# Opening of a two-layer decoder kernel: first weight tile in two loads, other order of its cast and products

## The chip, the cores and the metric

The kernel runs on one core of a Trainium2 chip. The metric is the device time of one execution in microseconds (us), lower is better. A core has five engines that run their own instruction streams and wait for each other by semaphores: TensorE (PE; its weight loads stand apart as PEld), VectorE (DVE), ScalarE (ACT), GpSimd (POOL) and SyncE (SP). Sixteen DMA engines, shared by all queues, move data between the chip's main memory and the core's on-chip memory.

## The reference

The input x is 256 x 1024 in float32. Two residual layers follow; each is an RMSNorm, one wide input projection, two groups of attention heads with gates, and an output projection that is added to x:

```
h    = rmsnorm(x, norm_gain[layer])
proj = h @ w_in_ab            # layer 0: 1024 x 4104; layer 1 uses w_in_cd
qa, ka, va, ga, qb, kb, vb, gb, fb = split_cols(proj, AB_SIZES)
...                           # two attentions; y gets their gated outputs
x    = x + y @ w_out_ab
```

What concerns us is the very beginning: the norm of x and the first 1024 columns of `h @ w_in_ab` (qa and ka, 512 columns each).

## The kernel before, in words

**Precision.** Every product is made in three: a float32 matrix is split into a high part (a cast to the engine's fast float32 form, made by ACT) and a low part (raw minus high, made by DVE), and `mm3` (lines 257 to 260) adds high x high, low x high and high x low. So a weight tile takes an ACT cast (line 120) and a DVE subtraction (line 121) before TensorE can use it. Both are in `wload`, which can do a tile in pieces.

**Loads.** All weight tiles are loaded by `wraws` (line 108) on SP's DMA queue, 512 KB each. The norm's scale is not applied to h before the projection, but to its result, so the projection can begin on the transposed x. `h_block(l, t, k, ps)` (lines 218 to 224) takes one transposed 128 x 128 block of x out of PSUM, row half t, column block k, times the norm's gain: ACT writes its high part `hth`, and DVE its low part `htl`.

**The opening** (from line 857 on) is written in program order for all engines. SP loads row half 0 of x (`xload(0)`), weight tile 0 (the rows of block k = 0, 1024 columns), row half 1 of x, tiles 1 to 3, and then tiles 4 to 7 into the rotating buffer `raw`; tiles 0 and 1 stand in the buffer `yth` and tiles 2 and 3 in `ytl`, so the profile calls their loads by these names. Here they are called w0, w1, w2, w3. POOL issues the loads of small parameters and, at line 908, of `wf`: 8 columns of the 1024 rows of w_in_ab, 32 bytes from each row, called the list load here.

`warm(n)` (lines 852 to 855) issues n matmuls of zeros with 512 columns, which nobody reads; `WARM = (5, 3)` says how many come ahead of the transposed gain column (line 875) and behind the four transposes of the first block group (`x_transp(0, 0)`, line 877).

Then come, by program order: `h_block` of blocks 0 and 1 of row half 0; the split of w0 in two pieces of 512 columns; the three products of w0's first piece with row half 0 (`mm_first(0, 0, 0)`); four transposes of row half 1 (line 883); `h_block` of blocks 0 and 1 of row half 1; the products of the second piece with row half 0; the split of w1; the six products of w0 with row half 1; and then w1's blocks, eight transposes, and w2 and w3 in the same way (lines 890 to 904). From line 905 on, a planner (`tick`) issues the work in units, with SP's loads waiting for free buffers.

Of the kernel before, what the change touches and what calls it, by code (L numbers as in the profile page):

```python
# [22 lines left out]
WF = 1040  # L23
NW = 5
AHEAD = 3
WARM = (5, 3)


@with_exitstack
def trunk_kernel(  # L30
# [6 lines left out]
    nc = tc.nc  # L37
    x, out = x[0], out[0]
    w_ab, wo_ab, w_cd, wo_cd = w_in_ab[0], w_out_ab[0], w_in_cd[0], w_out_cd[0]
# [20 lines left out]
    def xload(t):  # L60
        nc.sync.dma_start(xs[:, t, :], x[t * 128:(t + 1) * 128, :])
# [10 lines left out]
    def params(eng, rows):  # L72
        for i in rows:
            g = gains[i]
            eng.dma_start(
                prow[i:i + 1, :].rearrange("o (r d) -> o r d", r=2),
                bass.AP(tensor=g.tensor, offset=g.offset, ap=[[64, 1], [0, 2], [1, 64]]))

    def bcast(eng, name, src, n, t=None):
        t = cst.tile([128, n], F32, name=name) if t is None else t  # L80
        eng.dma_start(t, bass.AP(tensor=src.tensor, offset=src.offset,
                                       ap=[[0, 128], [1, n]]))
        return t
# [14 lines left out]
    def wraws(parts, nk, n, raw=None):  # L98
        if raw is None:
            raw = wraw.tile([128, WF], F32, name="raw")  # L100
        rv = raw[:, 0:nk * n].rearrange("p (k n) -> p k n", k=nk)
        for (c0, src) in parts:
            if isinstance(src, tuple):
                k0, f0 = src
                nc.gpsimd.tensor_copy(rv[:, :, c0:c0 + 4], wf[:, k0:k0 + nk, f0:f0 + 4])
                continue
            m = src.shape[1]
            last["sp"] = nc.sync.dma_start(rv[:, :, c0:c0 + m],
                                           src.rearrange("(k p) n -> p k n", p=128))
        return raw  # L110

    def wload(parts, nk, n, raw=None, pieces=1):
        if raw is None:
            raw = wraws(parts, nk, n)
        hi = wsp.tile([128, WF], F32R, name="whi")
        lo = wsp.tile([128, WF], F32R, name="wlo")
        m = nk * n // pieces
        for i in range(pieces):
            c = slice(i * m, (i + 1) * m)
            last["act"] = nc.scalar.copy(hi[:, c], raw[:, c])  # L120
            last["dve"] = nc.vector.tensor_tensor(out=lo[:, c], in0=raw[:, c], in1=hi[:, c].bitcast(F32),  # L121
                                    op=OP.subtract)
        return (hi[:, 0:nk * n].rearrange("p (k n) -> p k n", k=nk),
                lo[:, 0:nk * n].rearrange("p (k n) -> p k n", k=nk))
# [3 lines left out]
    tiles, wt, units, running = [], [], [], []  # L128
# [3 lines left out]
    def loads(limit):  # L132
        while len(wt) < len(tiles) and len(wt) - at["freed"] < limit:
            wt.append(wload(*tiles[len(wt)]))
# [11 lines left out]
    def tick(n=1):  # L146
        for _ in range(n):
            need, free, fn = units[at["unit"]]
            at["unit"] += 1
            while len(wt) < need:  # L150
                assert len(wt) - at["freed"] < NW
                wt.append(wload(*tiles[len(wt)]))
            fn()
            stages()
            at["freed"] += free
            loads(AHEAD)
# [37 lines left out]
    def x_transp(t, j):  # L194
        ps = pa.tile([128, 4, 128], F32, name="at", tag="ps")
        for i in range(4):
            k = 4 * j + i
            nc.tensor.transpose(ps[:, i, :], xs[:, t, k * 128:(k + 1) * 128], ident)
        return ps
# [18 lines left out]
    def h_block(l, t, k, ps):  # L218
        hth, htl = H["h"]
        c, g = slice(t * 128, (t + 1) * 128), gcol[:, 8 * l + k:8 * l + k + 1]  # L220
        nc.scalar.activation(hth[:, k, c], ps, AF.Copy, scale=g)
        nc.vector.scalar_tensor_tensor(out=htl[:, k, c], in0=ps, scalar=g,
                                       in1=hth[:, k, c].bitcast(F32),
                                       op0=OP.mult, op1=OP.subtract)
# [6 lines left out]
    def norm_r():  # L231
        ss = sml.tile([128, 2], F32, name="n_ss")
        for t in range(2):
            dump = act.tile([128, D], F32, name="yb")
            nc.scalar.activation(dump, xs[:, t, :], AF.Square, accum_out=ss[:, t:t + 1])  # L235
        m = sml.tile([128, 2], F32, name="n_m")
        nc.vector.tensor_scalar(m, ss, 1.0 / D, EPS, op0=OP.mult, op1=OP.add)
        em = sml.tile([128, 2], F32, name="n_em")
        nc.vector.tensor_scalar(em, m, EPS, None, op0=OP.mult)
        H["em"] = em  # L240
        y = rsqrt_tables(m, [128, 2])
        yield
        r = rsqrt_newton(m, y, [128, 2])
        rx = sml.tile([128, 2], F32, name="n_r")
        nc.vector.tensor_copy(rx, r)
        H["rx"] = rx
        yield
        pb = pa.tile([128, 512], F32, name="at", tag="ps")
        for t in range(2):
            nc.tensor.matmul(pb[:, t * 128:(t + 1) * 128], rx[:, t:t + 1].to_broadcast([128, 128]),  # L250
                             ident, start=True, stop=True)
        rb = act.tile([128, 256], F32, name="rb")
        nc.vector.tensor_copy(rb, pb[:, 0:256])
        H["rb"] = rb
# [7 lines left out]
    def bank():  # L262
        pt = pj.tile([128, 512], F32, name="pj", tag="ps")
        return pt
# [385 lines left out]
    def first():  # L650
        return proj2(w_ab, 0, (lambda ps: qk_heads(ps, 8, 0, qk_dst("qa", slice(0, 4))),
                               lambda ps: qk_heads(ps, 8, 4, qk_dst("ka", slice(0, 4)), room=True)))

    mm_first, run_first = first()
# [194 lines left out]

    wz = scr.tile([128, 512], BF16, name="sq", bufs=3)  # L850

    def warm(n):
        pt = bank()
        for _ in range(n):
            nc.tensor.matmul(pt, wz[:, 0:128], wz, start=True, stop=True)

    with tc.manual_schedule():
        nc.vector.memset(wz, 0.0)
        raws = []
        for n in ("yth", "ytl"):  # L860
            r = act.tile([128, 2, 1024], F32, name=n)
            raws += [r[:, 0, :], r[:, 1, :]]
        xload(0)
        wraws(*tiles[0], raws[0])
        xload(1)
        for i in range(1, 4):
            wraws(*tiles[i], raws[i])
        nc.gpsimd.iota(rel, pattern=[[-1, 256]], base=128, channel_multiplier=1,
                       allow_small_or_imprecise_dtypes=True)
        nc.vector.tensor_scalar(ident, rel[:, 0:128], 128.0, None, op0=OP.is_equal)  # L870
        nc.vector.memset(prow, 0.0)
        params(nc.gpsimd, (0, 4, 1, 5))
        warm(WARM[0])
        pgt = pv.tile([128, 512], F32, name="av", tag="ps")
        nc.tensor.transpose(pgt[:, 0:16], grow, ident[0:16, 0:16])
        nc.vector.tensor_copy(gcol, pgt[:, 0:16])
        p0 = x_transp(0, 0)
        warm(WARM[1])
        h_block(0, 0, 0, p0[:, 0, :])
        h_block(0, 0, 1, p0[:, 1, :])  # L880
        wt.append(wload(*tiles[0], raws[0], 2))
        mm_first(0, 0, 0)
        p1 = x_transp(1, 0)
        h_block(0, 1, 0, p1[:, 0, :])
        h_block(0, 1, 1, p1[:, 1, :])
        mm_first(0, 0, 1)
        wt.append(wload(*tiles[1], raws[1], 2))
        for j in range(2):
            mm_first(0, 1, j)
        for k in (2, 3):  # L890
            h_block(0, 0, k, p0[:, k, :])
            h_block(0, 1, k, p1[:, k, :])
        run_first(1)
        p0, p1 = x_transp(0, 1), x_transp(1, 1)
        wt.append(wload(*tiles[2], raws[2], 2))
        for k in (4, 5):
            h_block(0, 0, k, p0[:, k - 4, :])
            h_block(0, 1, k, p1[:, k - 4, :])
        run_first(2)
        wt.append(wload(*tiles[3], raws[3], 2))  # L900
        for k in (6, 7):
            h_block(0, 0, k, p0[:, k - 4, :])
            h_block(0, 1, k, p1[:, k - 4, :])
        run_first(3)
        at["freed"] += 3
        loads(3)
        bfor = bcast(nc.gpsimd, "bfor", b_forget, 8)
        nc.gpsimd.dma_start(wf, w_ab[:, 4096:4104].rearrange("(k p) n -> p k n", p=128))
        g = norm_r()
        next(g)  # L910
        running.append(g)
        at["freed"] += 1
        tick(1)
        biases((0, 1, 2, 3))
        tick(3)
        gain_cols(0)
# [63 lines left out]
```

## Time and profile before

| what | value |
|---|---|
| median of 3 runs | 278.92 us (276.66 to 279.52) |
| the profiled execution | 279.85 us, its span 278.1 us |
| PE busy, share of the span | 267.6 us, 96% |
| DVE busy | 212.2 us, 76% |
| ACT busy | 178.6 us, 64% |
| POOL busy | 7.2 us, 3% |
| chain that ended last | PE 74%, DMA 9%, DVE 8%, ACT 5% |
| granted TensorE clock, mean | 0.992 |

The span goes from the first to the last instruction of the program; the device time has about 1.7 us more around it. A busy PE is not one at its peak: the ends of its records overlap the next product. The chain is the sequence of work that ended last, followed backwards from the end, each step to what released it; work that is not in the chain was waiting for something in it or had time to spare.

### The profile page before, as it was taken

What the parts mean: (1) busy time and instruction counts of PE and PEld (TensorE: products, weight loads), DVE (VectorE), ACT (ScalarE), POOL (GpSimd) and SP (SyncE); (2) the same over time, 40 slices, a digit from 0 to 9 for tenths busy, and PEclk for the clock granted to TensorE, in tenths of its full rate; (3) what the DMA queues carried; (4) which work ended last, traced back from release to release, by engine and by line L of the source; (5) the groups of instructions that cost most, each with busy time, mean ns of one, the idle gap of its engine ahead of it and who ended that gap; (6) DMA issues with size and microseconds to landing.
All of it is one profiled execution on the core that took longest, in us unless ns stands there. A gap on an engine that the chain in (4) does not pass through costs nothing.

```text
span 278.1 us, 4629 instructions
## 1 busy us (share of the span) xinstructions
PE 267.6 (96%) x1665; PEld 225.7 (81%) x1665; DVE 212.2 (76%) x499; ACT 178.6 (64%) x394; POOL 7.2 (3%) x15
## 2 busy tenths in 40 slices
PE   7999999779999999999999999999999999999994
PEld 2876788558998889999788888888987899897784
DVE  2667998287877549999954988776999888698822
ACT  3469572576687557699742845465785798898500
POOL 6000003000000000000000000000000000000000
PEclk9999999979999999999999999999999999999999
DMA  7974864671444472205855367665508125307012
GB/s 238 202 317 128 225 194 150 195 239 24 148 143 116 118 222 78 77 8 165 247 195 165 90 213 242 212 181 182 167 1 272 35 73 175 132 4 222 5 75 76
DMA packets 26297, 41.38 MB, mean 149 GB/s; under 512 B 1665, under 2 KB 13330, under 8 KB 26274
## 3 DMA queue, kind: packets, MB, share of 16 engines
q1 hardware_dynamic: 26050, 41.04, 47.7%
q0 software_dynamic: 192, 0.04, 1.4%
q8 instruction: 13, 0.21, 0.3%
q14 instruction: 10, 0.08, 0.1%
q10 hardware_dynamic: 32, 0.01, 0.0%
HBM read 40.03 MB, written 1.05 MB: 148 GB/s over the span
## 4 chain that ended last, share of the span: by engine, by line
PE 74%; DMA 9%; DVE 8%; ACT 5%; issue 1%; SPq 1%; ACTq 0%
PE pj L258 21%; PE pj L259 20%; PE pj L260 20%; DMA ytl<-in_w_in_ab_dram 5%; DMA raw<-in_w_in_ab_dram 4%; DVE wlo L121 4%; PE at L509 3%; PE av L551 3%; ACT whi L120 2%; PE at L481 2%; PE at L377 2%; PE at L477 1%; DVE qk_m L344 1%; ACT yb L235 1%; DVE klo L395 1%
## 5 line engine op out<-in xcount | busy, mean ns | idle before, releaser
L121 DVE TENSOR_TENSOR wlo<-raw,whi 128x1024 fp32r<-128x1024 f32 (+1 forms) x70 | 85.2, 1223 | 21.8 <-ACT whi L120 18.3
L120 ACT CAST whi<-raw 128x1024 fp32r<-128x1024 f32 (+1 forms) x70 | 72.4, 1048 | 38.0 <-PE pj L259 20.4
L258 PE MATMUL pj<-whi,hth 128*128 128x512 f32 (+2 forms) x192 | 73.7, 384 | 0.6 <-ACT whi L120 0.5
L260 PE MATMUL pj<-wlo,hth 128*128 128x512 f32 (+2 forms) x192 | 71.2, 371 | 0.5 <-DVE wlo L121 0.5
L259 PE MATMUL pj<-whi,htl 128*128 128x512 f32 (+2 forms) x192 | 71.1, 370 | 0.0
L258 PEld LDWEIGHTS pj<-whi,hth 128*128 128x128 f32 x192 | 36.7, 191 | 8.5 <-ACT whi L120 2.0
L260 PEld LDWEIGHTS pj<-wlo,hth 128*128 128x128 f32 x192 | 36.6, 191 | 8.1 <-DVE wlo L121 1.6
L259 PEld LDWEIGHTS pj<-whi,htl 128*128 128x128 f32 x192 | 36.9, 192 | 5.6
L258 PE MATMUL pj<-hth,whi 128*128 128x256 f32 x128 | 37.0, 289 | 0.0
L260 PE MATMUL pj<-htl,whi 128*128 128x256 f32 x128 | 36.0, 281 | 0.0
L259 PE MATMUL pj<-hth,wlo 128*128 128x256 f32 x128 | 35.9, 281 | 0.0
L258 PE MATMUL pj<-whi,yth 128*128 128x512 f32 (+1 forms) x68 | 26.4, 388 | 0.0
L260 PE MATMUL pj<-wlo,yth 128*128 128x512 f32 (+1 forms) x68 | 25.9, 381 | 0.0
L259 PE MATMUL pj<-whi,ytl 128*128 128x512 f32 (+1 forms) x68 | 25.8, 380 | 0.0
L258 PEld LDWEIGHTS pj<-hth,whi 128*128 128x128 f32 x128 | 24.1, 188 | 0.7 <-issue 0.3
L259 PEld LDWEIGHTS pj<-hth,wlo 128*128 128x128 f32 x128 | 24.2, 189 | 0.0
L260 PEld LDWEIGHTS pj<-htl,whi 128*128 128x128 f32 x128 | 24.1, 188 | 0.0
L490 ACT ACTIVATE e<-e,mn 128x128 f32<-128x128 f32 x32 | 12.5, 390 | 8.9 <-DVE mn L486 8.9
L492 ACT ACTIVATE e<-e,mn 128x256 f32<-128x256 f32 x32 | 15.8, 495 | 0.0
L258 PEld LDWEIGHTS pj<-whi,yth 128*128 128x128 f32 x68 | 12.8, 188 | 2.7 <-issue 0.3
L260 PEld LDWEIGHTS pj<-wlo,yth 128*128 128x128 f32 x68 | 12.8, 188 | 2.6
L259 PEld LDWEIGHTS pj<-whi,ytl 128*128 128x128 f32 x68 | 12.8, 188 | 2.5
(167 smaller groups left out, 390.0 us busy)
## 6 DMA issues: line engine op xcount, KB each, us to landing
raw<-in_w_in_ab_dram SPq DMA_DIRECT2D x28, 512.0 KB, 7.9
raw<-in_w_in_cd_dram SPq DMA_DIRECT2D x26, 512.0 KB, 4.5
raw<-in_w_out_ab_dram SPq DMA_DIRECT2D x8, 512.0 KB, 3.7
raw<-in_w_out_cd_dram SPq DMA_DIRECT2D x8, 512.0 KB, 4.6
xs<-in_x_dram SPq DMA_DIRECT2D x2, 512.0 KB, 6.0
yth<-in_w_in_ab_dram SPq DMA_DIRECT2D x2, 512.0 KB, 7.0
ytl<-in_w_in_ab_dram SPq DMA_DIRECT2D x2, 512.0 KB, 12.7
out_dram<-xs SPq DMA_DIRECT2D x3, 256.0 KB, 2.0
```

The costliest lines, as they stand in the source:

```text
L120: last["act"] = nc.scalar.copy(hi[:, c], raw[:, c])
L121: last["dve"] = nc.vector.tensor_tensor(out=lo[:, c], in0=raw[:, c], in1=hi[:, c].bitcast(F32), op=OP.subtract)
L235: nc.scalar.activation(dump, xs[:, t, :], AF.Square, accum_out=ss[:, t:t + 1])
L258: nc.tensor.matmul(ps, ah, bh, start=first, stop=False)
L259: nc.tensor.matmul(ps, al, bh, start=False, stop=False)
L260: nc.tensor.matmul(ps, ah, bl, start=False, stop=last)
L377: nc.tensor.transpose(pt[:, i, :], qns[t][:, i * 128:(i + 1) * 128], ident)
L481: nc.tensor.matmul(scs[b][:, 128:384], q[r[b], i, :], k[r[b], ik, :], start=n == 0, stop=n == 2)
L490: nc.scalar.activation(e[:, 0:128], e[:, 0:128], AF.Exp, bias=mn[:, 0:1], scale=-1.0, accum_out=sm[:, 0:1])
L492: nc.scalar.activation(e[:, 128:384], e[:, 128:384], AF.Exp, bias=mn[:, 1:2], scale=-1.0, accum_out=sm[:, 1:2])
L509: nc.tensor.transpose(pt[:, i * 128:(i + 1) * 128], blocks[j + i], ident)
L551: nc.tensor.matmul(av[64 * b:64 * b + 64, i, t * 128:256], v[:, t, c:c + 64], p, start=t == 0, stop=t == 1)
```

## The change

The first weight tile is loaded by two instructions of 256 KB, one for each 512 columns. The transposes of row half 0 come behind one more zero product of 512 columns, and behind them come two of 512 and three of 128 columns in place of three of 512. `h_block` of block 1 of row half 0 moves from in front of w0's split to between the two blocks of row half 1, and the products of w0's second piece with row half 0 move in front of the transposes of row half 1.

```
-WARM = (5, 3)
+WARM = (5, 2, 3)
...
-    def warm(n):
+    def warm(n, m=0):
         pt = bank()
-        for _ in range(n):
-            nc.tensor.matmul(pt, wz[:, 0:128], wz, start=True, stop=True)
+        for c in (512,) * n + (128,) * m:
+            nc.tensor.matmul(pt[:, 0:c], wz[:, 0:128], wz[:, 0:c], start=True, stop=True)
...
         xload(0)
-        wraws(*tiles[0], raws[0])
+        for j in range(2):
+            nc.sync.dma_start(raws[0][:, j * 512:(j + 1) * 512], w_ab[0:128, j * 512:(j + 1) * 512])
         xload(1)
...
+        warm(1)
         p0 = x_transp(0, 0)
-        warm(WARM[1])
+        warm(*WARM[1:])
         h_block(0, 0, 0, p0[:, 0, :])
-        h_block(0, 0, 1, p0[:, 1, :])
         wt.append(wload(*tiles[0], raws[0], 2))
         mm_first(0, 0, 0)
+        mm_first(0, 0, 1)
         p1 = x_transp(1, 0)
         h_block(0, 1, 0, p1[:, 0, :])
+        h_block(0, 0, 1, p0[:, 1, :])
         h_block(0, 1, 1, p1[:, 1, :])
-        mm_first(0, 0, 1)
         wt.append(wload(*tiles[1], raws[1], 2))
```

## Rows read from the trace of the kernel before

**Rows 1.** Chain of waits, opening: start us, us, what
```profile
2.59 12.75 DMA ytl<-in_w_in_ab_dram
...
15.36 0.63 ACT whi L120
...
18.23 0.52 ACT whi L120
...
42.62 12.01 DMA raw<-in_w_in_ab_dram
```
**Rows 2.** Timeline of PE, 13.8 to 17: start us, us, instruction [idle before <-releaser]
```profile
14.89 1.04 PE L198 MATMUL at<-ident,xs 128*128 128x128 f32 x8
...
16.03 0.50 PE L258 MATMUL pj<-whi,hth 128*128 128x512 f32 x1
```
**Rows 3.** Stretches: us, busy us of each engine, PEclk, DMA share, GB/s
```profile
3.50:5.50 2.00, 1.68 (x8) 1.23 (x8) 0.24 (x2) 0.30 (x1) 2.00 (x4) 1.00 0.98 272
...
9.00:9.50 0.50, 0.50 (x4) 0.50 (x3) 0.00 (x0) 0.02 (x1) 0.00 (x0) 1.00 5.39 279
9.50:11.50 2.00, 2.00 (x7) 1.53 (x7) 1.03 (x3) 1.58 (x4) 0.00 (x0) 1.00 0.71 10
...
58.80:62.10 3.30, 3.30 (x18) 2.59 (x14) 3.18 (x17) 2.10 (x10) 0.00 (x0) 0.50 0.78 245
```
**Rows 4.** DMA queues, 9.0 to 9.8 us: queue, packets, MB, share of 16 engines
```profile
q0 software_dynamic: 16, 0.03, 473.9%
```
**Rows 5.** Timeline of ACT, 4 to 27 us: columns as in rows 2
```profile
5.20 0.37 ACT L221 ACTIVATE hth<-at,gcol 128x128 fp32r<-128x128 f32 x1 [3.18 <-PE at L198]
5.99 0.37 ACT L221 ACTIVATE hth<-at,gcol 128x128 fp32r<-128x128 f32 x1 [0.42 <-DVE htl L222]
6.27 1.14 ACT L120 CAST whi<-yth 128x512 fp32r<-128x512 f32 x2
9.48 0.37 ACT L221 ACTIVATE hth<-at,gcol 128x128 fp32r<-128x128 f32 x1 [2.07 <-PE at L198]
```
**Rows 6.** Timeline of PE, 4 to 12 us: columns as in rows 2
```profile
6.94 0.79 PE L258 MATMUL pj<-whi,hth 128*128 128x512 f32 x1 [0.50 <-ACT whi L120]
...
7.96 0.63 PE L260 MATMUL pj<-wlo,hth 128*128 128x512 f32 x1
8.39 1.05 PE L198 MATMUL at<-ident,xs 128*128 128x128 f32 x4
9.09 0.77 PE L258 MATMUL pj<-whi,hth 128*128 128x512 f32 x1
...
10.52 0.60 PE L258 MATMUL pj<-whi,hth 128*128 128x512 f32 x1
...
11.64 0.39 PE L259 MATMUL pj<-whi,htl 128*128 128x512 f32 x1
11.88 0.39 PE L260 MATMUL pj<-wlo,hth 128*128 128x512 f32 x1
```
**Rows 7.** Timeline of PE, 49 to 63 us: columns as in rows 2
```profile
52.23 0.66 PE L377 MATMUL at<-ident,e 128*128 128x128 f32 x4 [2.07 <-ACT v L404]
...
60.39 0.63 PE L259 MATMUL pj<-whi,htl 128*128 128x512 f32 x1
```
**Rows 8.** Timeline of SP's queue, 0 to 60 us: the issue of w1
```profile
2.11 0.43 SPq L108 DMA_DIRECT2D yth<-in_w_in_ab_dram  x1
```
**Rows 9.** Tile yth, loads of w0 and w1: from issue to landing
```profile
DMA to landing us min/median/max: 7.0/7.0/7.0
```
**Rows 10.** DMA queues, 24 to 40 us: as rows 4, here rows of 2 KB
```profile
q1 hardware_dynamic: 1900, 3.66, 81.2%
```
**Rows 11.** DMA queues, 6.5 to 9 us: as rows 4, here rows of 4 KB
```profile
q1 hardware_dynamic: 275, 1.01, 99.8%
q0 software_dynamic: 160, 0.01, 4.1%
```
**Rows 12.** The page, part 3, whole span: as rows 4
```profile
q0 software_dynamic: 192, 0.04, 1.4%
```

## The prediction

> **What bounds the kernel now.** I read the chain of waits first. Over the opening it doesn't run through TensorE: it stands on the load of w2 from its issue at 2.59 us to its landing at 15.34, goes on through ACT's cast at 15.36 and then through casts and subtractions, until an SP issue at 42.62 waits 12.01 us for another load [rows 1]. The reader is to see that whatever TensorE gains ahead of 15.34 has no place in this chain. The timeline around that point says how near the other work is: the last work ahead of w2's products, eight transposes, runs from 14.89 to 15.93, and the first product of w2 starts at 16.03, with the cast of 15.36 done [rows 2, 1]. TensorE thus has hardly any time to spare there, but it waits.
>
> Why does w2 land so late? The stretches answer: the DMA engines are full from 3.5 us on, but between 9.5 and 11.5 they move 10 GB/s [rows 3]. The queues of 9.0 to 9.8 us name the cause: 16 packets of POOL's queue (q0), 0.03 MB, hold the 16 engines for 473.9% of those 0.8 us, which is 4.739 x 0.8 = 3.8 us for each engine [rows 4]. That size is the list load's, 1024 rows of 32 bytes. It cuts w2 in two: some engines have finished w2 before it, the others bring their share after it.
>
> **Part 1, the cast in front of block 1, two loads.** Now ACT's `h_block` of block 1 waits for DVE and starts 0.79 us behind that of block 0 (5.20 and 5.99); the cast starts 0.28 us behind its predecessor, at 6.27 [rows 5], and the first real product follows at 6.94 [rows 6], 0.67 us behind the cast's start. The added zero product ahead of the transposes costs about 0.1 us: it fills the pause there and holds the first transpose back a little. So block 0 would start at 5.30, the cast at 5.58 and the first product at 6.25, which is 0.69 us earlier. The data must be there: the cast of 6.27 follows its predecessor without a pause, so w0 lands by then. If only just, half of it, 0.26 MB at the 272 GB/s of that stretch [rows 3], lands 0.96 us sooner, at 5.3. If the two halves arrive mixed, the cast waits until nearly 6.2 and this gain is zero. I take 0.69.
>
> **Part 2, the zero products.** The new group behind the transposes, two of 512 columns and three of 128, is 2.75 lengths where it was 3, and with the first real product 0.69 us earlier it fills the pause of 0.50 us that stands there now [rows 6]. The products of the opening follow each other by 0.42 to 0.43 us (7.96 to 8.39) and from 11.64 on 0.23 to 0.24 (11.64, 11.88) [rows 6]. The lower pace is that of the granted clock 0.50, which is 1.2 GHz of 2.4: at 58.8 to 62.1 us the column says 0.50 [rows 3] and a product of that size has the same 0.63 us there [rows 7]. (The column prints 1.00 for the opening because no change is recorded before it.) So the clock rises near 11 us, after products without a pause since 6.94. Without the pause it may rise at about the same time or up to right behind the first real product. In the second case eight products at 0.43 instead of 0.23 and four transposes at 0.70 start to start (8.39 to 9.09) instead of 0.52 (half of the eight in 1.04) save up to 2.3 us [rows 6, 2].
>
> **Part 3, the order of the products.** All six products of w0 with row half 0 now come in front of the transposes of row half 1. Before, three of them (9.09 to 10.52) covered ACT's block of row half 1, which started at 9.48 [rows 5, 6]. That cover is gone: after the transposes TensorE waits for one ACT operation of 0.37 us and its handover, 0.45 us together. By the old clock: 6.25 + 6 x 0.425 = 8.80, transposes to 9.85, ACT from 9.89, next product 10.30 where it was 10.52 [rows 6]. The gain of 0.69 shrinks to 0.22. On ACT three blocks now stand ahead of w1's cast: 9.89, 10.2, and the third waits for DVE as block 1 did, 0.79 us behind the first, so the cast starts at 9.89 + 0.79 + 0.28 = 10.96 where it was 9.48 + 0.79 + 0.28 = 10.55 [rows 5]. That delay is covered: w1's products would be ready at 10.96 + 0.67 = 11.63, and TensorE needs them at 11.9 (before: 11.88 + 0.23 = 12.11) [rows 6].
>
> **Part 4, one SP issue more.** Each later issue moves 0.43 us (the length of one) [rows 8]. The queue is full from 3.5 us on [rows 3], w2's data don't flow before w1 has landed, at 2.11 + 7.0 = 9.1 [rows 8, 9], so nothing waits for the issue. Rows of 2 KB in place of 4 KB: later the queue moves 1900 packets, 3.66 MB, in 81.2% of 16 us [rows 10], that is 109 ns each, so 16 of them per engine take 1.74 us; 4 KB take 162 ns (99.8% of 2.5 us, 1.01 MB) [rows 11], so eight take 1.30. The upper bound is 0.45 us. But w0's own stretch moves only 272 GB/s [rows 3], less than the 282 GB/s that the 2 KB rows reach when they flow (3.66 MB in 13.0 us), so the lower bound is zero. I take 0.1, near w0's own row.
>
> The rule in the Trainium skill, Perfetto Trace Analysis (DMA Optimizations), is that larger transfers use the memory better, and that splitting helps where DMA engines are idle. The share of 0.98 agrees with the first half of that warning, not with the condition of the second; by the rule alone the split would cost (an estimate: the 0.45 us of the upper bound) and not gain.
>
> **The sum.** TensorE reaches w2 between 0.2 us (old clock) and 0.2 + 2.3 = 2.5 us earlier. The wall at 15.34 moves by 0 to +0.45, I take +0.1. Gain on the end: none; change +0.1 us on the profiled execution's 279.85. That one stands 0.93 above the median of the runs shown, so on the median I leave it at 278.9. A lag or lead of TensorE is taken up later as well: at 52.23 it has waited 2.07 us [rows 7]. A longer wait ahead of w2 might also let the clock fall again, as at 58.8 [rows 3]; up to 2.07 us of that are covered by the same pause.
>
> **The rivals.**
>
> *Faster: w2 gets in front of the list load.* If every engine finishes w2 before its list packet, w2 lands near 9.9 rather than 15.34. For it: the engines' list packets start just when w2 flows, from 9.0 on [rows 3, 4]. Against: nothing in the change brings w2's data forward, and the split can only delay them. Then w3 is next, still behind the list load; its cast can start when it lands, about 1.3 us behind w2's old landing (eight 4 KB packets at 162 ns), 16.6, where the chain now has it at 18.1 to 18.2, behind w2's cast and the blocks of h [rows 1]. I take 1.4: 277.5 on the median. Chance 0.18.
>
> *Faster: the wall isn't one.* If in most executions the clock rises later than in this one, TensorE is late for w2, and the whole lead of part 2 with the 0.69 counts: 3.0 us, 275.9. For it: TensorE has only 0.1 us between its transposes and w2 [rows 2]. Against: it needs the profiled execution to be unusual. Chance 0.05.
>
> *Slower: w1 falls behind the list load.* w1 lands at 9.1 [rows 8, 9] and the list packets start in 9.0 to 9.5 [rows 3], so a slip of w1 by up to 0.4 us against POOL's queue is the point from which it decides; the split can bring 0 to 0.45. Then w1 lands at 9.1 + 3.8 = 12.9, or with the engines that hold the list longest at 15.34 - 1.3 = 14.0. ACT's cast and blocks of w1 (1.14, and some 1.84 up to the last block of the group) then end at 15.9 to 17.0, against a cast of w2 at 15.36: +0.5 to +1.7; by TensorE (twelve products at 0.23 and the transposes, 3.8 us) +1.3 to +2.5. I price it at 1.7: 280.6. Against it: of q0's 192 packets [rows 12], 160 run from 6.5 to 9 us, beside 275 of SP's [rows 11], and 16 are the list's [rows 4], so it has next to nothing while w0 flows. The Trainium skill, DMA: Bandwidth & Descriptors (Queues, rings and completion order), says that each engine takes turns between queues packet by packet; with smaller packets POOL's turns would come sooner per byte. In rows this matters only if q0 has work while w0 flows. Chance 0.13.
>
> *It doesn't do what it says:* the halves arrive mixed, the first product stays near 6.9; time as forecast, 278.9, chance 0.08.
>
> **How the numbers follow.** Forecast 0.56, and 0.08 of the last rival with the same time. A median of three runs scatters by some 1% here (276.66 to 279.52), and about 1%, 2.8 us, is what can be told from no change. Range: from 277.5 less half of that scatter, 276.1, up to the slower rival's upper end, 278.9 + 2.5, 281.4. Faster by over 1%: the second faster rival and a half of the first one's low side, 0.14. Slower by over 1%: the upper half of the slower rival, 0.07. Within 1%: 0.79.
>
> **What would show it.** Right: first real product near 6.25, the products of w0 at 0.23 spacing before 10 us, a longer wait of TensorE and ACT for the load of w2, and w2's cast still near 15.4. Wrong: w2's landing near 10, or w1's cast waiting for a load until 12 or later, or a chain that no longer contains the load of w2.

## The result, and the profile after

The changed kernel takes 280.45 us (median of 20 runs, 278.29 to 283.77), the kernel before 277.87 us (20 runs, 276.66 to 281.04). The ratio is 1.0077, 95% interval 1.0052 to 1.0102: slower by 2.1 us (0.0077 x 277.87). The ratio is not the quotient of the two medians, which is 1.0093 and would make the loss 2.6 us. Forecast were no change and 278.9 us, with a range of 276.1 to 281.4. The time lies in the range, but no change was forecast, and the loss is clear of the noise.

The profiled execution of the changed kernel took 278.29 us, the shortest of its twenty, so its span of 276.5 us says nothing about the loss. What it shows well is the opening. First the chain of waits (start us, us, what), which answers to [rows 1]:

```profile
3.06 13.13 DMA ytl<-in_w_in_ab_dram
...
16.22 0.63 ACT whi L120
...
19.08 0.52 ACT whi L120
...
42.17 9.03 DMA raw<-in_w_in_ab_dram
```

The chain still stands on the load of w2, as forecast. Its landing has moved from 15.34 to 16.19, and the casts behind it by the same 0.86. The forecast gave this term 0.1 us, and 0.45 at most.

The timeline of ACT shows the loads that the casts wait for (columns as in [rows 5]):

```profile
5.84 0.62 ACT L120 CAST whi<-yth 128x512 fp32r<-128x512 f32 x1 [0.25 <-DMA yth<-in_w_in_ab_dram]
7.65 0.62 ACT L120 CAST whi<-yth 128x512 fp32r<-128x512 f32 x1 [1.19 <-DMA yth<-in_w_in_ab_dram]
10.02 0.62 ACT L221 ACTIVATE hth<-at,gcol 128x128 fp32r<-128x128 f32 x2 [1.75 <-PE at L198]
10.80 0.37 ACT L221 ACTIVATE hth<-at,gcol 128x128 fp32r<-128x128 f32 x1 [0.16 <-DVE htl L222]
11.07 1.13 ACT L120 CAST whi<-yth 128x512 fp32r<-128x512 f32 x2
...
16.22 1.14 ACT L120 CAST whi<-ytl 128x512 fp32r<-128x512 f32 x2 [2.29 <-DMA ytl<-in_w_in_ab_dram]
```

The first half of w0 lands at 5.8 us, the second only at 7.6, where the whole of it was in by 6.27 before. On TensorE (as [rows 6] and [rows 2]) the same waits stand ahead of the products:

```profile
6.51 0.50 PE L258 MATMUL pj<-whi,hth 128*128 128x512 f32 x1 [0.52 <-ACT whi L120]
6.85 0.39 PE L259 MATMUL pj<-whi,htl 128*128 128x512 f32 x1
...
8.32 0.50 PE L258 MATMUL pj<-whi,hth 128*128 128x512 f32 x1 [0.58 <-ACT whi L120]
...
10.44 0.50 PE L258 MATMUL pj<-whi,hth 128*128 128x512 f32 x1 [0.46 <-ACT hth L221]
...
14.88 1.04 PE L198 MATMUL at<-ident,xs 128*128 128x128 f32 x8
16.89 0.51 PE L258 MATMUL pj<-whi,hth 128*128 128x512 f32 x1 [0.97 <-ACT whi L120]
```

The first real product starts at 6.51 rather than 6.94, and at 6.85 a product already takes 0.39 us, the length of the high clock level. All of that lead is gone by 14.88, where the eight transposes start as they did before (14.89), and the wait ahead of w2 has grown to 0.97 us.

Where does the slip begin? The DMA queues of 3.5 to 5.5 us (queue, packets, MB, share of 16 engines) tell it. Before:

```profile
q1 hardware_dynamic: 151, 0.54, 98.2%
```

and after:

```profile
q1 hardware_dynamic: 180, 0.32, 66.0%
```

The reader is to see three things: only a fifth more packets per us (75 and 90), far fewer bytes, and DMA engines that were full and now stand idle a third of the time. In this stretch rows arrive at a pace of their own, and a row of 2 KB is nearly as slow to come as one of 4 KB. The stretches (as [rows 3]) say the same in GB/s, 160 where it was 272:

```profile
3.50:5.50 2.00, 2.00 (x9) 1.31 (x9) 0.24 (x2) 0.27 (x1) 2.00 (x4) 1.00 0.66 160
...
9.50:11.50 2.00, 1.54 (x9) 1.02 (x8) 0.91 (x3) 1.32 (x4) 0.00 (x0) 1.00 1.11 143
```

The tile's landing row (as [rows 9]) puts w1 at 2.59 + 7.7 = 10.3 us, where it was 9.1:

```profile
DMA to landing us min/median/max: 7.7/7.7/7.7
```

The list load has not moved: its packets start from 9.0 us on in both profiles. So the slip leaves more of w2 behind it. By 9.5 us SP's queue had moved this much (DMA queues, 0 to 9.5 us), before and after:

```profile
q1 hardware_dynamic: 708, 2.60, 78.2%
```

```profile
q1 hardware_dynamic: 765, 2.29, 67.9%
```

The four loads ahead of w2 are 2.10 MB together. So 0.50 MB of what comes from w2 on had been moved by then before the change, and 0.19 MB after it.

### The profile page after: what moved, and what is told of

Its sections match the earlier page's. It is cut to its first block, busy times and chain, and to the rows that moved or that the text cites. A ratio compares the mean times of both kernels' runs of the same rounds, so it can differ in the third digit from the quotient of the medians.

```text
span 276.5 us, 4637 instructions
## 1 busy us (share of the span) xinstructions
PE 266.4 (96%) x1668; PEld 224.3 (81%) x1668; DVE 211.8 (77%) x499; ACT 178.3 (64%) x394; POOL 7.2 (3%) x15
## 4 chain that ended last, share of the span: by engine, by line
PE 76%; DMA 8%; DVE 7%; ACT 5%; issue 1%; SPq 1%; ACTq 0%
PE pj L258 21%; PE pj L259 20%; PE pj L260 20%; DMA ytl<-in_w_in_ab_dram 5%; DVE wlo L121 4%; PE at L509 3%; DMA raw<-in_w_in_ab_dram 3%; PE av L551 3%; ACT whi L120 2%; PE at L377 2%; PE at L481 2%; PE at L477 1%; DVE qk_m L344 1%; ACT yb L235 1%; ACT e L492 1%
```

## The experiments

Each kernel has one edit against the kernel before, the changed one or another of the table. The ratio is to the kernel before, run on the same chip, with its 95% interval; a kernel that ran once has none. The time column can't be divided by its first row: the kernel before took 278.78 us beside e1, e2, e3 and e5, 277.78 beside e4, e6, e8 and e9, and 278.63 beside e10 and e11. Landings are from the profile of each.

| kernel | w1 lands | w2 lands | time us | ratio |
|---|---|---|---|---|
| before | 9.1 | 15.3 | 277.87 | 1 |
| the change | 10.3 | 16.2 | 280.45 | 1.0077 (1.0052 to 1.0102) |
| e1 split only | 10.1 | 17.9 | 280.85 | 1.0077 (1.0043 to 1.0111) |
| e2 change, one load | 9.1 | 15.3 | 278.00 | 0.9983 (0.9949 to 1.0017) |
| e3 change, halves by rows | 9.4 | 15.0 | 278.90 | 1.0009 (0.9981 to 1.0037) |
| e5 POOL's loads late | 8.9 | 10.2 | 276.24 | 0.9935 (0.9899 to 0.9971) |
| e6 split, POOL's loads late | 9.7 | 11.0 | 276.98 | 0.9930 (0.9901 to 0.9960) |
| e8 order and zeros, one load, POOL's late | 8.7 | 10.5 | 276.75 | 0.9939 (0.9905 to 0.9972) |
| e4 list load late | 9.3 | 10.3 | 275.79 | 0.9921 (0.9890 to 0.9951) |
| e11 w1 split, not w0 | 9.1 | 15.4 | 277.73 | 0.9986 (0.9957 to 1.0015) |
| e9 later issues held back | 9.1 | 17.3 | 279.81 | one run |
| e10 all of x first | 8.7 | 15.4 | 278.31 | one run |

**Which part of the change costs: the loads, or the order and the clock?** e1 has the two loads and nothing else of the change:

```
-        wraws(*tiles[0], raws[0])
+        for j in range(2):
+            nc.sync.dma_start(raws[0][:, j * 512:(j + 1) * 512], w_ab[0:128, j * 512:(j + 1) * 512])
```

> The kernel before with one edit: w0 in two loads of 512 columns; order and zero products as before. Theory PACKETS (from 3.5 to 5.5 us the DMA engines are held up by each row they carry, not by its bytes: before 151 packets of 4 KB at a share of 98%, after 180 of 2 KB at 66%; 128 rows more push all later loads back): w0's second half lands at 7.3 to 7.7 us, w1 at 10.0 to 10.4, w2 later than 15.8, ratio to before 1.004 to 1.010, like the whole change. Theory ORDER (the loss comes from the new order on TensorE and ACT and from the clock): loads as late, but ratio 0.998 to 1.002.

e2 is the changed kernel with these two lines turned back.

> The changed kernel with w0 in one load again; new order and new zero products stay. PACKETS: w0 at 6.2, w1 at 9.1, w2 at 15.3 us, ratio to before 0.996 to 1.002. ORDER: ratio 1.004 to 1.010, with waits of TensorE for ACT behind the transposes of row half 1 (0.45 us) and a low clock more often.

Measured: 1.0077 for the two loads alone, the same as for the whole change, and 0.9983 for the rest without them. So the loads carry the whole loss, and the order and the zero products neither win nor lose anything that can be measured (the interval of e2 leaves room for a gain of 0.5%). The chain of e1 and its cast of w2 show the landing of w2, the wall that all work behind it waits for, further out than in the profile of the change:

```profile
3.06 14.84 DMA ytl<-in_w_in_ab_dram
```

```profile
17.92 1.14 ACT L120 CAST whi<-ytl 128x512 fp32r<-128x512 f32 x2 [4.69 <-DMA ytl<-in_w_in_ab_dram]
```

Behind the wait of 3.37 us for it, TensorE's granted clock is at its low level, 0.50, which may add to the loss. Its row at 18.59, and the stretch (as [rows 3]) that follows:

```profile
18.59 0.79 PE L258 MATMUL pj<-whi,hth 128*128 128x512 f32 x1 [3.37 <-ACT whi L120]
```

```profile
19.50:21.00 1.50, 1.50 (x5) 1.20 (x5) 1.32 (x5) 0.92 (x4) 0.00 (x0) 0.50 0.43 175
```

In e2 w2 lands where it did before, and the lead of TensorE (its eight transposes start at 14.28, before: 14.89) ends as a wait of 0.71 us ahead of a product that starts at 16.02 (before: 16.03). Two rows, of the chain and of PE:

```profile
2.59 12.74 DMA ytl<-in_w_in_ab_dram
```

```profile
16.02 0.50 PE L258 MATMUL pj<-whi,hth 128*128 128x512 f32 x1 [0.71 <-ACT whi L120]
```

**Is it the second instruction or the smaller rows?** e3 keeps two loads, each of 64 whole rows:

```
-            nc.sync.dma_start(raws[0][:, j * 512:(j + 1) * 512], w_ab[0:128, j * 512:(j + 1) * 512])
+            nc.sync.dma_start(raws[0][j * 64:(j + 1) * 64, :], w_ab[j * 64:(j + 1) * 64, 0:1024])
```

> The changed kernel with w0 in two loads again, but each of 64 rows of 4 KB in place of 128 rows of 2 KB: as many instructions as in the change, as many packets as before. PACKETS: w1 lands at 9.1 to 9.5 us, ratio to before 0.997 to 1.003. Theory ISSUE (one more DMA instruction and its completion cost the time): w1 at 10.0 or later, ratio 1.004 to 1.010.

Its queue of 3.5 to 5.5 us and its landing row of w1 (3.07 + 6.3 = 9.4):

```profile
q1 hardware_dynamic: 148, 0.49, 87.2%
```

```profile
DMA to landing us min/median/max: 6.3/6.3/6.3
```

As many loads as in the change, as many rows as before, and the loss is gone (1.0009). What delays the loads behind w0 is the rows, not the instruction. The second instruction isn't free for w0 itself: it is complete at 7.3 (the first cast starts at 7.33), about 1 us later than before and as late as in e1 (7.31). But 0.49 MB moved in the stretch, where e1 has 0.34, and w1 is only 0.3 later than before.

**Do small rows cost wherever they stand?** e11 splits w1 in place of w0, in the same way.

> The kernel before with w1, not w0, in two loads of 512 columns. w1 flows from 7 to 9 us, where packets of 4 KB took 160 ns. Theory PLACE (small rows cost much only in the held-up stretch of 3.5 to 5.5 us): w0 lands at 6.3, w1 at 9.1 to 9.3, w2 at 15.1 to 15.6 us, ratio 0.998 to 1.003. Theory SIZE (128 packets more cost 1 us wherever they stand): w1 at 10.0 or later, ratio 1.004 to 1.010.

No: w1 lands at 9.1 as before and the ratio is 0.9986. Here is its queue from 7.0 to 8.5 us, where the halves of w1 flow, 267 packets in 1.5 us, which is 178 per us:

```profile
q1 hardware_dynamic: 267, 0.53, 89.9%
q0 software_dynamic: 115, 0.01, 5.0%
```

So the same split is free where packets of 2 KB come at 178 per us, and costs where they come at 90, as in the stretch of w0.

**What holds up that stretch?** Three suspects: POOL's own loads, which are being issued then; SP, which is issuing later loads; and the time itself, whatever is loaded. e5 holds POOL's loads behind w2's cast by a one-column copy that waits for it, and moves nothing else:

```
         wt.append(wload(*tiles[2], raws[2], 2))
+        nc.gpsimd.tensor_copy(wf[:, 0, 0:1], wt[2][0][:, 0, 1023:1024].bitcast(F32))
+        nc.gpsimd.dma_start(wf, w_ab[:, 4096:4104].rearrange("(k p) n -> p k n", p=128))
+        params(nc.gpsimd, (0, 4, 1, 5))
+        bfor = bcast(nc.gpsimd, "bfor", b_forget, 8)
```

> The kernel before with all of POOL's loads (gains, forget bias, list load) issued only behind the cast of w2, by a copy of one column on POOL that waits for it; nothing else moved. Theory POOL HOLDS (POOL's loads make both the slow stretch of 3.5 to 5.5 us and the hole of 9.5 to 11.5): packets of 4 KB at 160 ns from 2.5 us on, w0 lands before 5.6, w1 before 8.0, w2 before 9.6 us; ratio to before 0.990 to 0.996. If only the hole is POOL's: w0 still at 6.2, w1 at 9.1, w2 at 10.0, ratio 0.993 to 0.998. If the wall at w2's landing isn't one: ratio 0.998 to 1.002.

Its two stretches:

```profile
3.50:5.50 2.00, 1.71 (x8) 1.25 (x8) 0.24 (x2) 0.33 (x1) 0.00 (x0) 1.00 1.00 289
...
9.50:11.50 2.00, 2.00 (x9) 1.48 (x9) 1.41 (x4) 1.90 (x5) 0.00 (x0) 1.00 1.04 295
```

The hole at 9.5 is filled (295 GB/s for 10), the slow stretch stays (289 for 272). POOL's loads make the one and not the other. The second case of the expectation holds, and at 0.9935 the wall is shown to be one. e9 tries SP: a write of one column into w2's buffer, behind the first block of h, holds back all issues from w2 on.

```
         h_block(0, 0, 0, p0[:, 0, :])
+        nc.vector.memset(raws[2][:, 0:1], 0.0)
+        for i in (2, 3):
+            wraws(*tiles[i], raws[i])
```

> The kernel before, with SP's issues of w2 and of all later tiles held until the first low part of h is written (about 6 us), by a write of one column into w2's buffer on DVE. Theory ISSUING (the slow stretch from 3.5 to 5.5 us comes from SP generating descriptors of later loads while earlier ones flow): packets of 4 KB at 160 ns in that stretch, over 190 of them, w0 lands at 5.3 to 5.6 us. Otherwise: some 75 packets per us as before, w0 at 6.2 to 6.4.

```profile
q1 hardware_dynamic: 174, 0.61, 99.2%
```

174 packets in 2 us, neither the 150 of the one theory nor the 190 of the other, and w0 is cast at 6.42, no sooner than before (6.27). How much of the difference is chance shows e11, where nothing has changed up to then:

```profile
q1 hardware_dynamic: 166, 0.61, 93.7%
```

e2, with w0 in one load as well, has 144. SP's issuing isn't the cause either, or only a small part of it. The held loads now come behind the list load, and w2 lands at 17.3. The single time of 279.81 fits the wall, but lies within the times of the kernel before (276.99 to 280.90) and shows nothing by itself. e10 loads row half 1 of x in front of w0:

```
         xload(0)
-        wraws(*tiles[0], raws[0])
         xload(1)
+        wraws(*tiles[0], raws[0])
```

> The kernel before with row half 1 of x loaded ahead of w0. Theory TIME (the slow stretch lies at 3.5 to 5.5 us whatever is loaded): some 75 packets of 4 KB per us there, now of x, x's second half lands at 5.9 to 6.4 and w0 at 7.4 to 7.9 us. Theory MATRIX (the first rows read from the weight matrix are slow): x's second half lands by 5.3, packets of the stretch over 90 per us until then, and slow ones behind it.

```profile
q1 hardware_dynamic: 228, 0.82, 101.6%
```

With x in the stretch of 3.5 to 5.5 us, 228 packets flow, 114 per us, at a full share. The second half of x is in by 5.3, and w0, now behind it, lands at 7.2. So the time isn't the cause by itself either, and none of the three suspects explains the slow stretch. The slow rows go with the load of w0, the first rows that are taken from the weight matrix: it still needs 1.83 us (landings at 5.34 and 7.17), where x needed 1.31 in its place (4.03 to 5.34). In its own place it needed 2.25 (4.00 to 6.25), so a part may be the place's. Why these rows are slow no run settles.

**Slip or wall?** The slip of 1 us could cost by itself, because everything behind comes later, or only because the list load then holds more of w2. e6 is e5 with w0 in two loads of 512 columns.

> The kernel before with POOL's loads behind w2's cast, as in the run with POOL's loads late (ratio 0.9935), and w0 in two loads of 512 columns. Theory WALL (the split's slip of about 1 us costs only because it lets the list load catch more of w2): without the list load in the way w1 lands near 10.0 and w2 near 11.3 us, neither is waited for on the path, ratio 0.993 to 0.996. Theory SLIP (every later load comes 1 us later, and that alone moves the end): ratio 0.998 to 1.001.

```profile
q1 hardware_dynamic: 183, 0.32, 51.7%
```

The slip is there (0.32 MB in the stretch again, w1 at 9.7 for 8.9 in e5), and the ratio is 0.9930, no worse than e5's 0.9935. Theory WALL holds: where the load of w2 is not on the path, the split costs nothing that can be measured (both intervals are some 0.3% to either side).

**Does the new order gain once the wall is gone?** e8 is e5's edit on the changed kernel with one load.

> The changed kernel's order and zero products, w0 in one load, POOL's loads behind w2's cast. With the wall at w2 gone, TensorE's lead of the new order (0.6 us ahead of w2 in the run with one load) may count: ratio 0.988 to 0.9925. If casts and subtractions set the pace from there on and not TensorE, the order adds nothing: 0.992 to 0.995.

0.9939 against e5's 0.9935: no gain to be seen. Two products of w0 in the profile of e8 (timeline of PE):

```profile
8.34 0.63 PE L258 MATMUL pj<-whi,hth 128*128 128x512 f32 x1
8.77 0.63 PE L259 MATMUL pj<-whi,htl 128*128 128x512 f32 x1
```

and in that of e5:

```profile
8.85 0.39 PE L259 MATMUL pj<-whi,htl 128*128 128x512 f32 x1
9.08 0.39 PE L260 MATMUL pj<-wlo,hth 128*128 128x512 f32 x1
```

With the zero products e8 still has 0.63 us, the length of the low clock level, where e5, which has a pause of 0.90 us ahead of its first real product, is already at the length of the high one. In the profiles of the change (6.85) and of e2 (0.40 us at 7.35), which have the same zero products, the high level came as early as in e5. So the zero products do not fix when the clock rises, and a pause there does not keep it from rising. These are single executions; what share of them rises early in either kernel was not measured. ACT's cast of w2 starts at 14.49 in e8 and at 12.62 in e5, in both without a wait for the load, and the order's own part in the result stays unseparated.

**The version to keep.** e4 moves the list load alone, and leaves the small loads early:

```
         wt.append(wload(*tiles[2], raws[2], 2))
+        bfor = bcast(nc.gpsimd, "bfor", b_forget, 8)
+        nc.gpsimd.tensor_copy(wf[:, 0, 0:1], wt[2][0][:, 0, 1023:1024].bitcast(F32))
+        nc.gpsimd.dma_start(wf, w_ab[:, 4096:4104].rearrange("(k p) n -> p k n", p=128))
```

> The kernel before with the list load alone issued behind w2's cast; POOL's small loads stay early. If the list load alone is the wall: w2 lands near 10.0 us, ratio 0.991 to 0.996, like the run with all of POOL's loads late. If the small loads hold the queue as well: w2 at 11 or later, ratio above 0.996.

```profile
DMA to landing us min/median/max: 7.7/7.7/7.7
```

w2 lands at 2.59 + 7.7 = 10.3, and at 275.79 us (ratio 0.9921) it beats both kernels. The list load alone was the wall.

## Why the prediction was wrong, point by point

- **What bounds the opening** was right. The chain after still stands on w2, the four kernels that let w2 land by 11.0 gain 0.61% to 0.79%, and TensorE's lead without the split (e2) ends in a longer wait there.
- **Part 1** (0.69 us) was right in kind and too large: 0.43 (6.94 to 6.51), because half of w0 lands at 5.8 and not at 5.3. It had no price for the other half, which lands at 7.6: the second piece's products wait for it until 8.32.
- **Part 2** was right at its upper end in the profiled execution: a product of 0.39 us stands at 6.85, so the clock was up by the first real products. Its 2.3 us is a wrong sum: eight products at 0.20 and 0.18 for the transposes are 1.8. The lead at w2 that was built on it, 0.2 to 2.5 us, came to nothing in the change (14.88 for 14.89), where TensorE waited for w0's second half instead; without the split (e2) it was 0.6. That it was the zero products that brought the clock up is not shown (e8 has them and rises late).
- **Part 3** was right on the lost cover: it shows as 0.46 us of waiting at 10.44 (forecast 0.45). That w1's cast starts at 11.07, near the 10.96 forecast, is luck: the forecast had six products without a pause at the low clock, and the run had six at the high one with a wait for w0's second half in between.
- **Part 4 is the step that failed**: "The upper bound is 0.45 us. But w0's own stretch moves only 272 GB/s ... so the lower bound is zero. I take 0.1". The term measured 1.2 us at w1 and 0.9 (profile of the change) to 2.6 (e1) at w2, and 2.1 us in the time. The mistake lies in the reading of [rows 3] and [rows 10]: I took 2 KB rows at the pace of a later stretch, and took 272 GB/s below 282 as proof that packets don't set the pace. A share of 0.98 with slow bytes meant the contrary: packets that were held up, at 208 ns each (0.982 x 32 us / 151) for 145 when they flow (0.998 x 40 us / 275 in [rows 11]). With the split the engines stood idle between packets instead. A price in bytes can't be carried from a stretch where packets flow to one where they are held up. The 0.45 itself mixes two ways of counting: 109 ns is time over packets, 162 time over bytes. With 109 and 145 the bound is 0.59, still half of what w1 lost. The count of packets there (75 per us) was to be had before the run, and 128 more of them at that pace are 1.7 us (128 / 75), which would have been the upper bound to state.
- **The slower rival** named the right place (a slip against the list load) and the wrong tile. The list load hardly held w1, which landed at 10.3 and not at 12.9 to 14.0; it was more of w2 that fell behind it. That its price of 1.7 us, worked out for w1, came near the 2.1 measured is luck. Its chance was 0.13.
- **The faster rivals**: w2 did not get in front of the list load by the change. e4 and e5 got it there by other means, and gained 2.2 and 1.8 us (0.0079 and 0.0065 x 278); 1.4 had been forecast for that case.
- The Trainium skill, Perfetto Trace Analysis (DMA Optimizations), says that splitting may let some parts start sooner and may help where DMA engines are idle, and that larger transfers do better. The change's rows agree with it: the first half comes 0.4 us sooner (5.8 for 6.27) and the whole 1.3 us later, where the engines had been full (0.98). e11, where the same split is free at a share of 0.90, says that the size alone doesn't decide it.

## What to carry to other kernels

Price a split load by packets, not by bytes alone, and take the pace from the stretch where the new packets will stand: if the DMA share is full while GB/s is low, as it was for w0 here, packets are held up there, and more of them may cost their full number. Before a lead is bought upstream, find the landing that the chain stands on and ask what delays it; here 32 KB read as 1024 pieces of 32 bytes held each DMA engine for 3.8 us, and to issue them later was worth more (e4: 0.9921) than the whole reordering (e2: 0.9983).

## What the runs showed that I had not expected

- The first 128 rows read from the weight matrix come slowly whoever else is issuing: 0.54 MB in 2 us before, 0.58 MB (157 packets) with POOL silent, 0.61 MB with SP's later issues held and 0.61 MB in e11 with neither, against 0.82 MB when x stands there. The same load one place later (w1) comes at 407 GB/s and more.
- The execution times of one kernel follow the mean granted clock. Of 81 executions of the kernel before, beside e1 to e11, 28 have a clock of 0.997 or more and average 277.3 us, 49 have 0.991 to 0.994 and average 278.8, and four have 0.988 and average 280.7. Of the changed kernel's twenty, four fall in the first of these groups and average 279.2 us (1.9 above), eight in the second with 279.7 (0.9 above), so a loss remains at the same clock. But eight more are at 0.981 to 0.987 and average 282.2, so low clock is part of the loss as well. e1's profile shows one way to it, the low stretch behind the wait of 3.37 us for w2. The prediction had named it: "A longer wait ahead of w2 might also let the clock fall again". Whether the eight had that wait is not known, because only one execution was profiled. e4 has eleven of its twelve in the first group, with 275.8 us.
